# Moving a kernel's SBUF tiles to multiples of 256 bytes: padding and pool order in a hybrid encoder layer

## The chip, the cores and the metric

The kernel runs on one core of a Trainium2 chip. The metric is the device time of one execution in microseconds (us). Three runs of the kernel before gave 811.33, 809.4 and 811.11 us, so the median is 811.11 us; a change is called faster or slower where it differs from no change by more than about 0.3 per cent, 2.4 us.

## What is computed

One layer of an encoder for 256 tokens of width 1024, in float32: a half-step SwiGLU network, then a projection that feeds a multi-head latent attention (MLA) and a bidirectional state-space scan (SSD), whose gated results are added back, and a second half-step SwiGLU network.

```python
def reference(x, ...):
    x = x + 0.5 * swiglu(rmsnorm(x, ffn1_norm[l]), ffn1_w_gate[l], ffn1_w_up[l], ffn1_w_down[l])
    h = rmsnorm(x, mix_norm[l])
    u = h @ w_in[l]
    c_q, c_kv, k_pe, z, xbc, dt_f, dt_b, g_a, g_b = jnp.split(u, split_idx, axis=-1)
    a = mla(c_q, c_kv, k_pe, ...)
    m = bi_mamba2(xbc, z, dt_f, dt_b, ...)
    merged = jax.nn.sigmoid(g_a) * (a @ w_attn_branch[l]) + jax.nn.sigmoid(g_b) * (m @ w_ssm_branch[l])
    x = x + merged @ w_out[l]
    x = x + 0.5 * swiglu(rmsnorm(x, ffn2_norm[l]), ffn2_w_gate[l], ffn2_w_up[l], ffn2_w_down[l])
    return x
```

swiglu(h) is (silu(h @ w_gate) * (h @ w_up)) @ w_down, with 2816 hidden columns.

## The kernel before

**Layout.** Activations lie transposed: a tile has 128 partitions (features) and 256 tokens along them. All large products have a weight block of 128 x 128 as the stationary operand, which LDWEIGHTS puts into TensorE, and the activations as the moving operand of a MATMUL.

**Splitting.** TensorE reads float32r here, and to keep float32 accuracy every operand is split in two parts, hi and lo, and a product is the sum of three: hi by hi, hi by lo and lo by hi. An activation's two parts lie side by side, 256 columns of hi and then 256 of lo, in tiles with the axes [P, k, 2, T]: xs (normed input of a stage), hs (hidden activations of a feed-forward network) and ms (output of the state-space scan). Each k takes 2048 bytes of a partition. `wload` (L112 to L125) brings a weight block by DMA into one of four buffers raw, ScalarE copies it into one of four buffers whi (through `copy`, L94) and VectorE puts raw minus whi into one of four buffers wlo (through `tt`, L97). Three pairs of tensors for the first part of the input projection are loaded early into a pool of their own, pre.

**Two matmul loops.** `wstat` (L135 to L143) issues three MATMULs of 256 columns for each weight block: whi by hi (L141), whi by lo (L142), wlo by hi (L143), and each has its own LDWEIGHTS. It makes the input projection (ps_in0 from pre, with the xs of the mixing norm; ps_in1 from whi and wlo), the attention branch (ps_ab), the second half of the scan's branch (ps_sb, which reads ms) and the output projection (ps_o2, which the profile shows as ps_o). `wstat2` (L145 to L156) issues two for each block: wlo by hi, 256 columns (L153, or L156 for the first block of a sum), and whi by hi and lo at once, 512 columns (L154). It makes the two feed-forward networks (ps_gu and ps_d) and the gates and the first half of the scan's branch (ps_half). Here one block's work in `wstat` is called a triple, and in `wstat2` a pair; each covers 768 columns.

**Order of the work.** First network (22 blocks f of ps_gu, then 8 blocks d of ps_d), input projection, then a plan of attention heads, scan pairs and projections that is sorted by hand-set keys, the branches, the output projection, the second network. Each engine works through its own queue in program order; the DMAs of weights are issued by SP.

**Where tiles lie.** Pools take space in a partition from below in the order in which they are opened, and pools with side="right" from above. In the kernel before the pool const is opened first (L81), and raw, w, x, xn and small follow. Later come h and ev (feed-forward networks), or mix and then m0 or attn (mixing part), and from above pre, or ssd in its place. ms and mpb are the last tiles taken from mix (L508 and L509). A tile's buffers are a multiple of 256 bytes apart for raw, whi, wlo, xs, hs and ms (4352, 4352, 4352, 16384, 45056 and 16384 bytes).

Of the kernel before, what the change touches and what calls it, by code (L numbers as in the profile page):

```python
# [8 lines left out]
F32 = mybir.dt.float32  # L9
F32R = mybir.dt.float32r  # L10
# [5 lines left out]
P = 128  # L16
T = 256
# [5 lines left out]


RAWB, WB = 4, 4
NMM, NPL, NG = 3, 2, 3
EB, PRB, QKB = 4, 2, 2

# [44 lines left out]
def build(ctx, tc, A, out, dbg=None):  # L73
# [4 lines left out]
    def pool(name, bufs=1, **kw):  # L78
        return tc.tile_pool(name=name, bufs=bufs, **kw)

    cp = ctx.enter_context(pool("const"))  # L81
    rawp = ctx.enter_context(pool("raw", RAWB))
    wp = ctx.enter_context(pool("w", WB))
    xp = ctx.enter_context(pool("x"))
    xnp = ctx.enter_context(pool("xn", 2))
    sm = ctx.enter_context(pool("small", 2))

    def dump(name, ap):
        if name in dbg:
            nc.sync.dma_start(dbg[name], ap)  # L90
# [120 lines left out]
    def xn_tiles():  # L211
        return xnp.tile([P, KD, 2, T], F32R, tag="xs", name="xs")
# [164 lines left out]
    with ExitStack() as es:  # L377
        mp = es.enter_context(pool("mix", reuse_waits="tile"))
# [7 lines left out]
            return ps_g.tile([P, 512], F32, tag="g", name=name)  # L386


        cqh = mp.tile([P, 3, T], F32R, name="cqh")
        cql = mp.tile([P, 3, T], F32R, name="cql")  # L390
        ckh = mp.tile([P, 2, T], F32R, name="ckh")
# [113 lines left out]
        dump("acs", acs)  # L505

        as_ = xn_tiles()
        ms = mp.tile([P, 8, 2, T], F32R, name="ms")  # L508
        mpb = mp.tile([P, 8, T], F32, name="mpb")  # L509

        m0_es.close()
        at_es = es.enter_context(ExitStack())
# [392 lines left out]
```

## Time and profile before

| | us |
|---|---|
| median of three runs | 811.11 |
| the profiled execution | 809.85 |
| its span, first to last instruction | 808.1 |
| TensorE matmul (PE) busy | 786.8 |
| VectorE (DVE) busy | 625.0 |
| ScalarE (ACT) busy | 493.6 |

The profiled execution took 1.75 us more than its span and 1.26 us less than the median. PE is TensorE with its MATMULs, PEld its LDWEIGHTS, which overlap them. A MATMUL is shown from its start to a modelled end, and the next begins before that end; so the pace of a stream of MATMULs is read from the distance of their starts, not from the busy time or from the duration of one. Names such as ps_gu<-xs,whi are the tile written, then the tiles read.

### The profile page before, as it was taken

How to read it: one execution, taken by the hardware profiler on the slowest of the kernel's cores; microseconds unless marked ns; L12 is line 12 of the kernel's file. 1: busy time of each engine (PE TensorE's matmuls, PEld its weight loads, DVE VectorE, ACT ScalarE, POOL GpSimd, SP SyncE). 2: the span in 40 equal slices, each digit the busy share in tenths (PEclk: the TensorE clock that was granted, in tenths of full speed). 3: DMA queues.
4: the chain of work that ended last, by engine and by line, in shares of the span. 5: the costliest groups of instructions: out<-in, count | busy, mean ns of one | idle time of the engine just before them, and what ended most of it. 6: DMA issues, size and time to landing. Idle time of an engine off the chain costs nothing.

```text
span 808.1 us, 13739 instructions
## 1 busy us (share of the span) xinstructions
PE 786.8 (97%) x5232; PEld 700.4 (87%) x5232; DVE 625.0 (77%) x1276; ACT 493.6 (61%) x866; POOL 0.2 (0%) x4
## 2 busy tenths in 40 slices
PE   5999999999998999999999999999999999999998
PEld 4888888888998998988988887888998888888887
DVE  5899987667797986897898678767787877777553
ACT  6667665555367659569667675567455655655442
POOL 0000000000000000000000000000000000000000
PEclk9999999999999999999999999999999999999999
DMA  7667774667134443322325514441755465564772
GB/s 262 207 196 241 237 237 145 180 187 233 40 104 162 132 135 103 108 79 89 100 82 159 176 54 146 137 135 56 232 172 191 161 204 181 189 188 138 197 211 75
DMA packets 39090, 126.46 MB, mean 156 GB/s; under 512 B 4464, under 2 KB 5872, under 8 KB 39024
## 3 DMA queue, kind: packets, MB, share of 16 engines
q1 hardware_dynamic: 38592, 124.69, 48.6%
q10 hardware_dynamic: 432, 0.89, 0.3%
q8 instruction: 41, 0.67, 0.3%
q14 instruction: 25, 0.20, 0.1%
HBM read 124.52 MB, written 1.05 MB: 155 GB/s over the span
## 4 chain that ended last, share of the span: by engine, by line
PE 87%; DVE 6%; ACT 5%; issue 1%; DMA 1%; ACTq 0%
PE ps_gu L154 20%; PE ps_d L154 10%; PE ps_gu L153 9%; PE ps_half L154 5%; PE ps_d L153 5%; PE ps_in L142 4%; PE ps_in L143 4%; PE ps_in L141 4%; PE ps_y L700 3%; PE ps_half L153 2%; PE ps_sc L613 2%; PE ps_o L640 1%; PE ps_gu L156 1%; PE ps_pl L682 1%; DVE wlo L97 1%; PE ps_pT L630 1%
## 5 line engine op out<-in xcount | busy, mean ns | idle before, releaser
L97 DVE TENSOR_TENSOR wlo<-raw,whi 128x1024 fp32r<-128x1024 f32 (+4 forms) x256 | 289.1, 1131 | 75.5 <-ACT whi L94 74.6
L94 ACT ACTIVATE whi<-raw 128x1024 fp32r<-128x1024 f32 (+4 forms) x256 | 251.6, 986 | 145.4 <-PE ps_d L154 51.2
L154 PE MATMUL ps_gu<-xs,whi 128*128 128x512 f32 x704 | 243.8, 400 | 7.8 <-DVE xs L100 7.7
L153 PE MATMUL ps_gu<-xs,wlo 128*128 128x256 f32 x616 | 173.3, 281 | 1.8 <-DVE wlo L97 1.8
L154 PEld LDWEIGHTS ps_gu<-xs,whi 128*128 128x128 f32 x704 | 127.2, 190 | 32.2 <-ACT whi L94 7.2
L153 PEld LDWEIGHTS ps_gu<-xs,wlo 128*128 128x128 f32 x616 | 117.4, 191 | 6.4 <-DVE wlo L97 2.3
L154 PE MATMUL ps_d<-hs,whi 128*128 128x512 f32 x352 | 122.5, 393 | 0.0
L142 PE MATMUL ps_in<-xs,whi 128*128 128x256 f32 x368 | 105.3, 286 | 0.6 <-DVE xs L100 0.6
L143 PE MATMUL ps_in<-xs,wlo 128*128 128x256 f32 x368 | 105.0, 285 | 0.0
L141 PE MATMUL ps_in<-xs,whi 128*128 128x256 f32 x368 | 104.3, 283 | 0.0
L153 PE MATMUL ps_d<-hs,wlo 128*128 128x256 f32 x336 | 94.7, 282 | 0.0
L154 PEld LDWEIGHTS ps_d<-hs,whi 128*128 128x128 f32 x352 | 65.2, 188 | 13.8
L142 PEld LDWEIGHTS ps_in<-xs,whi 128*128 128x128 f32 x368 | 70.1, 190 | 1.2 <-DVE xs L100 0.8
L143 PEld LDWEIGHTS ps_in<-xs,wlo 128*128 128x128 f32 x368 | 70.1, 191 | 0.5 <-issue 0.3
L141 PEld LDWEIGHTS ps_in<-xs,whi 128*128 128x128 f32 x368 | 70.1, 190 | 0.1
L153 PEld LDWEIGHTS ps_d<-hs,wlo 128*128 128x128 f32 x336 | 63.1, 188 | 0.7
L94 ACT ACTIVATE gu<-ps_gu 128x512 f32<-128x512 f32 x44 | 26.1, 592 | 35.0 <-PE ps_gu L154 35.0
L100 DVE SCALAR_TENSOR_TENSOR xz<-ps_in,vec,xz 128x254 f32<-128x254 f32 (+1 forms) x96 | 44.7, 475 | 1.6 <-ACT xz L530 0.9
L154 PE MATMUL ps_half<-xs,whi 128*128 128x512 f32 x128 | 44.9, 399 | 0.0
L97 DVE TENSOR_TENSOR gu<-ps_gu,gu 128x512 f32<-128x512 f32 x44 | 30.3, 688 | 16.5 <-ACT gu L94 15.9
L97 DVE TENSOR_TENSOR E<-E,cb 128x512 f32<-128x512 f32 x48 | 32.0, 685 | 2.4 <-ACT E L691 1.5
L276 ACT ACTIVATE sg<-gu 128x256 f32<-128x256 f32 x44 | 18.1, 416 | 24.4 <-DVE gu L97 24.3
(232 smaller groups left out, 1375.5 us busy)
## 6 DMA issues: line engine op xcount, KB each, us to landing
raw<-in_w_gu SPq DMA_DIRECT2D x86, 512.0 KB, 3.9
raw<-in_w_in SPq DMA_DIRECT2D x62, 512.0 KB, 4.1
raw<-in_w_d SPq DMA_DIRECT2D x32, 384.0 KB, 3.2
raw<-in_w_d SPq DMA_DIRECT2D x32, 320.0 KB, 3.4
raw<-in_w_sb SPq DMA_DIRECT2D x16, 512.0 KB, 4.2
raw<-in_w_qkv SPq DMA_DIRECT2D x8, 544.0 KB, 3.8
raw<-in_w_ab SPq DMA_DIRECT2D x8, 512.0 KB, 3.8
raw<-in_w_o SPq DMA_DIRECT2D x8, 512.0 KB, 3.8
```

The costliest lines, as they stand in the source:

```text
L94: S.activation(dst, src, AF.Copy, scale=scale)
L97: V.tensor_tensor(out=dst, in0=a, in1=b, op=op)
L100: V.scalar_tensor_tensor(out=dst, in0=a, scalar=s, in1=b, op0=op0, op1=op1)
L141: TE.matmul(ps, pc.hi[:, w], xh, start=first and i == 0, stop=False)
L142: TE.matmul(ps, pc.hi[:, w], xl, start=False, stop=False)
L143: TE.matmul(ps, pc.lo[:, w], xh, start=False, stop=last and i == len(ks) - 1)
L153: TE.matmul(ps[:, 0], pc.lo[:, w], xs[:, k0 + i, 0], start=False, stop=False)
L154: TE.matmul(ps, pc.hi[:, w], xs[:, k0 + i], start=a, stop=b)
L156: TE.matmul(ps[:, 0], pc.lo[:, w], xs[:, k0 + i, 0], start=False, stop=False)
L276: S.activation(sg, gu[:, 0], AF.Silu)
L613: TE.matmul(sc[:, t * T:(t + 1) * T], qk[:HD, t * P:(t + 1) * P], qk[:HD, T:2 * T], start=True, stop=True)
L700: TE.matmul(py[64 * j:64 * j + 64, a:b], st[c, d][:, hh_], M[i][:, j, a:b], start=n == 0, stop=n == 3)
```

## The change

Two pools of padding are opened, below raw (96 floats, 384 bytes of each partition) and behind small (120 floats), and one at the right side (8 floats, 32 bytes). The pool const moves behind the pool xn. In the pool mix, ms and mpb become the first tiles. Nothing else is changed: every engine has the same instructions in the same order with the same waits, and only their addresses differ.

```diff
+PAD0, PAD1, PAD2 = 96, 120, 8
...
-    cp = ctx.enter_context(pool("const"))
+
+    ctx.enter_context(pool("pad0")).tile([P, PAD0], F32, name="pad0")
     rawp = ctx.enter_context(pool("raw", RAWB))
     wp = ctx.enter_context(pool("w", WB))
     xp = ctx.enter_context(pool("x"))
     xnp = ctx.enter_context(pool("xn", 2))
+    cp = ctx.enter_context(pool("const"))
     sm = ctx.enter_context(pool("small", 2))
+    ctx.enter_context(pool("pad1")).tile([P, PAD1], F32, name="pad1")
+    ctx.enter_context(pool("pad2", side="right")).tile([P, PAD2], F32, name="pad2")
...
+        ms = mp.tile([P, 8, 2, T], F32R, name="ms")
+        mpb = mp.tile([P, 8, T], F32, name="mpb")
         cqh = mp.tile([P, 3, T], F32R, name="cqh")
...
         as_ = xn_tiles()
-        ms = mp.tile([P, 8, 2, T], F32R, name="ms")
-        mpb = mp.tile([P, 8, T], F32, name="mpb")
```

The first buffer of each tile, in bytes from the start of a partition, and the remainder after division by 256:

| tile | before | remainder | after | remainder |
|---|---|---|---|---|
| raw | 25632 | 32 | 16896 | 0 |
| whi | 43040 | 32 | 34304 | 0 |
| wlo | 60448 | 32 | 51712 | 0 |
| x | 77856 | 32 | 69120 | 0 |
| xs | 86048 | 32 | 77312 | 0 |
| hs | 124064 | 160 | 124928 | 0 |
| ms | 138304 | 64 | 124928 | 0 |
| mpb | 154688 | 64 | 141312 | 0 |
| cqh, cql, ckh, ckl | 124064 and up | 160 | 149504 and up | 0 |
| whi, wlo of pre | 180192, 204768 | 224 | 180160, 204736 | 192 |
| xz, xd, E of the scan | 186336 and up | 224 | 186304 and up | 192 |
| eye, msk4 | 22816, 23328 | 32 | 116384, 116896 | 160 |
| st1, st2 | 136256, 137280 | 64 | 161696, 162720 | 160 |
| nacc, nsq | 118816, 119840 | 32 | 119200, 120224 | 160 |
| gu of the networks | 169120 | 160 | 169984 | 0 |

## The prediction

> **What bounds the kernel now.** I read the page first: its busy times and the chain that ended last.
>
> ```profile
> PE 786.8 (97%) x5232; PEld 700.4 (87%) x5232; DVE 625.0 (77%) x1276; ACT 493.6 (61%) x866; POOL 0.2 (0%) x4
> ...
> PEclk9999999999999999999999999999999999999999
> ...
> PE 87%; DVE 6%; ACT 5%; issue 1%; DMA 1%; ACTq 0%
> ```
>
> TensorE works in 97% of the span, makes up 87% of the chain, and its clock is granted in full in every slice. So what the change is worth hangs on the pace at which matmuls follow each other; transfers, ScalarE and VectorE lie beside them. The view of the groups gives the counts of the streams that the change touches.
>
> ```profile
> L154 PE MATMUL ps_gu<-xs,whi 128*128 128x512 f32 x704 | 243.8, 400 | 7.8 <-DVE xs L100 7.7
> L154 PE MATMUL ps_d<-hs,whi 128*128 128x512 f32 x352 | 122.5, 393 | 0.0
> L142 PE MATMUL ps_in<-xs,whi 128*128 128x256 f32 x368 | 105.3, 286 | 0.6 <-DVE xs L100 0.6
> L154 PE MATMUL ps_half<-xs,whi 128*128 128x512 f32 x128 | 44.9, 399 | 0.0
> L154 PE MATMUL ps_half<-ms,whi 128*128 128x512 f32 x64 | 21.9, 393 | 0.0
> L142 PE MATMUL ps_ab<-xs,whi 128*128 128x256 f32 x64 | 18.2, 286 | 0.0
> L142 PE MATMUL ps_o<-xs,whi 128*128 128x256 f32 x64 | 18.1, 283 | 0.0
> L142 PE MATMUL ps_sb<-ms,whi 128*128 128x256 f32 x64 | 17.8, 278 | 0.0
> ```
>
> L154 is issued once in a pair: 704 + 352 + 128 + 64 = 1248 pairs. L142 is issued once in a triple: 368 + 64 + 64 + 64 = 560 triples. The idle time before them is next to nothing, but the durations are modelled and overlap, so they don't give a pace. The pace comes from the timeline, from starts one whole tile apart. First `wstat`, with 24 matmuls from one row to the next: ps_o, whose moving operand xs starts 32 bytes behind a multiple of 256; then ps_sb, with the same code and the same buffers whi and wlo, whose moving operand ms starts 64 bytes behind one; then ps_in0, with xs at 32 but weights from pre, at 224.
>
> ```profile
> 604.98 0.28 PE L141 MATMUL ps_o<-xs,whi 128*128 128x256 f32 x1
> ...
> 610.74 0.28 PE L141 MATMUL ps_o<-xs,whi 128*128 128x256 f32 x1
> ```
>
> ```profile
> 572.76 0.28 PE L141 MATMUL ps_sb<-ms,whi 128*128 128x256 f32 x1
> ...
> 578.41 0.28 PE L141 MATMUL ps_sb<-ms,whi 128*128 128x256 f32 x1
> ```
>
> ```profile
> 209.49 0.28 PE L141 MATMUL ps_in<-xs,whi 128*128 128x256 f32 x1
> ...
> 212.32 0.28 PE L141 MATMUL ps_in<-xs,whi 128*128 128x256 f32 x1
> ```
>
> ps_o: 5.76 us over 48 matmuls, 120.0 ns each, 360 ns a triple. ps_sb: 5.65 us over 48, 117.7 ns, 353 a triple. ps_in0: 2.83 us over 24, 117.9 ns, 354 a triple. The work is the same and the addresses differ; the pace differs by 2%. That is the one thing in this trace that says an address matters at all.
>
> Now `wstat2`. L156 comes once for each sum, so its starts are 8 pairs apart in ps_gu and ps_half, and 22 in ps_d.
>
> ```profile
> 120.59 0.28 PE L156 MATMUL ps_gu<-xs,wlo 128*128 128x256 f32 x1
> 123.36 0.28 PE L156 MATMUL ps_gu<-xs,wlo 128*128 128x256 f32 x1
> 126.19 0.28 PE L156 MATMUL ps_gu<-xs,wlo 128*128 128x256 f32 x1
> ```
>
> ```profile
> 152.78 0.28 PE L156 MATMUL ps_d<-hs,wlo 128*128 128x256 f32 x1
> 160.49 0.28 PE L156 MATMUL ps_d<-hs,wlo 128*128 128x256 f32 x1
> ```
>
> ```profile
> 435.29 0.28 PE L156 MATMUL ps_half<-ms,wlo 128*128 128x256 f32 x1
> ...
> 452.05 0.28 PE L156 MATMUL ps_half<-ms,wlo 128*128 128x256 f32 x1
> ```
>
> ps_gu takes turns: 2.77 us for one sum, 2.83 us for the next, so 346.3 and 353.8 ns a pair, 350.0 in the mean, at addresses that are equal modulo 256 throughout. ps_d: 7.71 / 22 = 350.5. ps_half with ms: 16.76 us over 48 pairs, 349.2. So here the start of the moving operand (32, 160, 64) hardly shows, while the same stream has two paces of its own.
>
> **The change, part by part.** *Instructions.* Nothing is added, removed or moved, and no wait changes; all that can change is how fast an instruction runs at its new address.
>
> *The triples.* ms, at 64, is the only moving operand of a split product that starts at a multiple of 64 bytes before. After the change xs, hs and ms all do. I take the pace of the nearest row, ps_sb's 117.7, for all triples that now go at 120.0: the 560, less 64 of ps_sb, less 48 of ps_in0 (6 tiles of 8 blocks), which have the lower pace already. That is 448 x 3 = 1344 matmuls x 2.3 ns = 3.1 us, all on the path, since TensorE doesn't wait in these stretches. The bounds: no gain, if the pace follows something else; and below nothing, if the 192 matmuls of ps_sb lose their lead, + 192 x 2.3 = 0.4 us.
>
> *The pairs.* By the same rule they take the pace of ps_half with ms, 349.2. (704 + 128) x 0.8 + 352 x 1.3 = 0.7 + 0.5 = 1.1 us. The 128 pairs of ps_half with xs are counted like ps_gu, whose operand they share. The bounds are ps_gu's own two paces. If all go at 346.3: 832 x 3.7 + 352 x 4.2 + 64 x 2.9 = 3.1 + 1.5 + 0.2 = 4.7 us less. If all go at 353.8: 832 x 3.8 + 352 x 3.3 + 64 x 4.6 = 3.2 + 1.2 + 0.3 = 4.6 us more. I take the value of ms, since it is the only row with an operand of the new kind.
>
> *The weights.* whi and wlo start at 32 modulo 64 everywhere in this trace (pre at 224 too), so no row shows a load of a block that starts at a multiple of 64. I take nothing for it; as a bound towards faster I take as much again as for the moving operand, and as a bound towards slower the pace 353.8 above.
>
> *The tiles the change doesn't reach.* pre and the scan's tiles go from 224 to 192, eye, msk4, st1 and st2 end at 160, and the attention's small tiles stay off 256. ps_in0, the one split product among the readers of pre, runs at the lower pace already. I take nothing for them.
>
> *VectorE and ScalarE.* Do their instructions depend on the start? Operations of one size:
>
> ```profile
> L97 DVE TENSOR_TENSOR sg<-sg,gu 128x256 f32<-128x256 f32 x44 | 18.3, 419 | 3.8 <-ACT sg L276 3.8
> L97 DVE TENSOR_TENSOR nacc<-nacc,nsq 128x256 f32<-128x256 f32 x21 | 8.8, 418 | 0.5 <-ACT nsq L236 0.4
> L97 DVE TENSOR_TENSOR mpb<-mpb,gt 128x256 f32<-128x256 f32 x16 | 5.7, 420 | 0.1
> ```
>
> sg starts at 160, nacc at 32, mpb at 64, and they take 419, 418 and 420 ns: no. For ScalarE I assume the same. And can they keep up with a faster TensorE? The tightest long stretch, from the windows:
>
> ```profile
> 40.00:136.00 96.00, 96.00 (x551) 83.66 (x550) 85.12 (x123) 63.99 (x99) 0.00 (x0) 1.00 0.67 214
> ```
>
> VectorE (the figure ahead of x123) is busy 85.12 of 96 us, ScalarE (ahead of x99) 63.99. A stretch that is 1% shorter leaves VectorE nearly 10 us to spare, so it does not become the bound.
>
> *Transfers.* The raw buffers and x, too, start elsewhere. Weight blocks arrive ahead of need. Only x is waited for:
>
> ```profile
> 1.65 7.54 DMA x<-in_xt
> ```
>
> No row shows the same transfer at two starts, so I take nothing; one hundredth of this piece, either way, would be 0.08 us.
>
> *The sum.* 3.1 + 1.1 = 4.2 us less. The profiled execution of 809.85 us (a span of 808.1 and 1.75 around it) would become 805.6; the median of 811.11 us lies 1.26 above that execution and would become 806.9, 0.5% less.
>
> **The rivals.** *It is the relative start, not the multiple (no difference).* ps_o's triples, at 120.0, have a moving operand at 32 and weights at 32, so both start at the same place modulo 256. ps_sb has 64 and 32, ps_in0 32 and 224: both differ, and they run at 117.7 and 117.9. After the change xs, whi and wlo stand at 0, again the same place, so ps_in1, ps_ab, ps_o and ps_gu keep their pace, and ms joins them at 0: + 192 x 2.3 ns = 0.4 us, plus 64 pairs x 0.8 = 0.05. That gives 811.6 us. For it speaks ps_in0, which is fast though both its operands start at 32 modulo 64; this is the strongest row against my forecast. Against it speaks ps_d, at 160 with weights at 32, which is no faster than ps_gu's mean. [...]
>
> *The slow beat everywhere (slower).* ps_gu shows that one stream at fixed addresses has two paces, and that it goes over from the one to the other at each new sum. Which of them a stream falls into may follow from how the reads of the weights and of the moving operand meet. With all three operands at the same place modulo 256 all pairs may settle at 353.8 and all triples at 120.0: 4.6 + 0.4 = 5.0 us more, 816.1 us. It decides from the point where more than half of the pairs that now go faster stay at 353.8, since then 2.4 us are lost. For it speaks that ps_o, with the same place for both, is locked at 120.0; against it, that ps_gu has both operands at 32 as well and is locked only half of the time.
>
> *The fast beat everywhere.* The far end of my own case: pairs at 346.3 and triples at 117.7, 4.7 + 3.1 = 7.8 us less, 803.3 us. It needs ps_gu to lose its slow turn altogether.
>
> **How the numbers follow.** The forecast with its far end has a chance of 0.45: 806.9 us, and by itself 803 to 809. No difference has 0.36, slower 0.19. The measurement tells 0.3%, 2.4 us, from no change; the forecast's 4.2 lies outside of that, the relative start inside, the slow beat outside. The range: at the low end twice the forecast's gain, for weight loads that gain as much as the moving operand, 2 x 4.2 = 8.4 us, 802.7, rounded down to 802; at the high end the slow beat, cut short a little at 815. About one in ten is left out on each side.
>
> **What would show it right or wrong.** In the profile after: starts of ps_o's L141 24 matmuls apart by 2.82 to 2.83 us instead of 2.88 is the forecast's first term; by 2.88 still, with ps_sb up from 2.82 to 2.88, is the relative start. In ps_gu, L156 every 2.79 us in the mean is the second term; 2.77 each time is the fast beat, 2.83 each time the slow one. ps_in0 should stay at 2.83. VectorE's 418 to 420 ns and the transfer of x should stay. The prediction is wrong if the pace of the streams stays and the time moves, for then something else depends on the address; or if weight loads at 0 give a pace outside of 346 to 354 a pair, which no row of before shows.

## The result and the profile after

| | before | after |
|---|---|---|
| median of 20 runs, us | 809.73 | 810.61 |
| lowest and highest | 808.43, 811.35 | 809.59, 812.46 |
| span of the profiled execution | 808.1 | 808.6 |

The ratio is 1.0013 with a 95% interval of 1.0007 to 1.0019: 0.9 us more, which lies within the 0.3 per cent that count as no difference. Forecast were 4.2 us less. (The median of three runs that the forecast started from, 811.11, lies 1.4 us above that of twenty; this moves the forecast time, not the difference.)

The page of the kernel after has TensorE in the same place: busy in 97% of the span, its clock granted in full (0.999 in the mean).

```profile
span 808.6 us, 13739 instructions
...
PE 787.4 (97%) x5232; PEld 699.9 (87%) x5232; DVE 625.3 (77%) x1276; ACT 493.9 (61%) x866; POOL 0.2 (0%) x4
...
PEclk9999999999999999999999999999999999999999
```

So the pace of the streams decides here too. The timeline of the kernel after, first for triples (L147 is their first MATMUL; 24 matmuls are 8 triples): ps_in0, ps_sb, ps_o.

```profile
209.35 0.28 PE L147 MATMUL ps_in<-xs,whi 128*128 128x256 f32 x1
...
212.07 0.28 PE L147 MATMUL ps_in<-xs,whi 128*128 128x256 f32 x1
...
572.08 0.28 PE L147 MATMUL ps_sb<-ms,whi 128*128 128x256 f32 x1
...
577.84 0.28 PE L147 MATMUL ps_sb<-ms,whi 128*128 128x256 f32 x1
...
604.70 0.28 PE L147 MATMUL ps_o<-xs,whi 128*128 128x256 f32 x1
...
610.46 0.28 PE L147 MATMUL ps_o<-xs,whi 128*128 128x256 f32 x1
```

ps_o: 5.76 us over 48 matmuls, 120.0 ns each, as before. ps_sb: 5.76 over 48, 120.0, up from 117.7. ps_in0: 2.72 over 24, 113.3, down from 117.9; nothing before the change went as fast. Now the pairs (L162, once in each sum): ps_gu 8 pairs apart, ps_d 22, ps_half with ms 48 from the first row to the last.

```profile
119.79 0.28 PE L162 MATMUL ps_gu<-xs,wlo 128*128 128x256 f32 x1
122.56 0.28 PE L162 MATMUL ps_gu<-xs,wlo 128*128 128x256 f32 x1
125.38 0.28 PE L162 MATMUL ps_gu<-xs,wlo 128*128 128x256 f32 x1
...
151.96 0.28 PE L162 MATMUL ps_d<-hs,wlo 128*128 128x256 f32 x1
159.72 0.28 PE L162 MATMUL ps_d<-hs,wlo 128*128 128x256 f32 x1
...
434.96 0.28 PE L162 MATMUL ps_half<-ms,wlo 128*128 128x256 f32 x1
...
451.74 0.28 PE L162 MATMUL ps_half<-ms,wlo 128*128 128x256 f32 x1
```

ps_gu still takes turns at 2.77 and 2.82. ps_d has 7.76 / 22 = 352.7 ns a pair in place of 350.5, ps_half 16.78 / 48 = 349.6 in place of 349.2.

To see whether this makes up the time, I take for each stream the mean distance from each start to the next (distances over 300 ns, which are waits, left out), times three for a triple and summed over both matmuls for a pair. Where a number below is called a mean, it is this one; it holds the short pauses between sums too.

| stream | count | before, ns | after, ns | difference, us |
|---|---|---|---|---|
| ps_d, first and second network | 176, 176 pairs | 350.3, 350.3 | 352.2, 353.1 | +0.3, +0.5 |
| ps_sb | 64 triples | 353.4 | 360.0 | +0.4 |
| ps_in0 | 48 triples | 357.4 | 348.5 | -0.4 |
| ps_half with ms | 64 pairs | 349.1 | 349.8 | 0.0 |
| ps_gu, first and second network | 352, 352 pairs | 352.0, 349.6 | 351.8, 349.5 | -0.1, 0.0 |
| ps_in1 | 320 triples | 367.5 | 367.1 | -0.1 |
| ps_ab | 64 triples | 365.6 | 365.7 | 0.0 |
| ps_o | 64 triples | 363.4 | 363.4 | 0.0 |

The sum is 0.6 us more, beside the 0.9 of the medians and the 0.5 between the two profiled spans. Four streams changed their pace. In three of them (ps_d, ps_sb, ps_half with ms) the operand moved relative to its weights; ps_in0 kept its distance and fell into another rhythm. The streams whose operand and weights moved together (xs with whi and wlo) kept it.

### The profile page after: what moved, and what is told of

Its sections match the earlier page's. It is cut to its first block, busy times and chain, and to the rows that moved or that the text cites. A ratio compares the mean times of both kernels' runs of the same rounds, so it can differ in the third digit from the quotient of the medians.

```text
span 808.6 us, 13739 instructions
## 1 busy us (share of the span) xinstructions
PE 787.4 (97%) x5232; PEld 699.9 (87%) x5232; DVE 625.3 (77%) x1276; ACT 493.9 (61%) x866; POOL 0.2 (0%) x4
## 4 chain that ended last, share of the span: by engine, by line
PE 85%; DVE 7%; ACT 6%; issue 1%; DMA 1%; ACTq 0%
PE ps_gu L160 20%; PE ps_d L160 10%; PE ps_gu L159 9%; PE ps_half L160 5%; PE ps_d L159 5%; PE ps_in L148 4%; PE ps_in L149 4%; PE ps_in L147 3%; PE ps_y L706 3%; PE ps_half L159 2%; PE ps_sc L619 2%; DVE wlo L103 1%; PE ps_o L646 1%; PE ps_gu L162 1%; PE ps_pT L636 1%
## 5 line engine op out<-in xcount | busy, mean ns | idle before, releaser
L160 PE MATMUL ps_d<-hs,whi 128*128 128x512 f32 x352 | 123.3, 398 | 0.0
L147 PE MATMUL ps_in<-xs,whi 128*128 128x256 f32 x368 | 104.2, 283 | 0.0
L147 PEld LDWEIGHTS ps_in<-xs,whi 128*128 128x128 f32 x368 | 70.0, 190 | 0.1
```

The costliest lines, as they stand in the source:

```text
L147: TE.matmul(ps, pc.hi[:, w], xh, start=first and i == 0, stop=False)
L160: TE.matmul(ps, pc.hi[:, w], xs[:, k0 + i], start=a, stop=b)
```

## The experiments

Three theories stood at the start. *Relative start*: what counts is the distance, modulo 256 bytes, from the start of the weights to the start of the moving operand, and a distance of 0 is a slow case. *Multiple*: the forecast's reason, a start at a multiple of 64 or 256 is faster by itself. *Chance*: a stream falls into one of its rhythms whatever its starts.

**Starts alone.** A kernel of only triples and pairs, in sections that take any start (in bytes modulo 256: moving operand, whi, wlo). The layer is left out. This kernel and the three others of sections ran once each.

```python
SECS = [('t', 0, 0, 0), ('p', 0, 0, 0), ('t', 4, 0, 0), ..., ('t', 32, 32, 32), ('p', 32, 32, 32), ...]
```

> The kernel leaves out the layer: it loads x, two tiles of weights and one of moving data, runs sections of split matmuls in the loops' own forms (triples of three 256-column matmuls, pairs of 256 and 512) at chosen starts, and writes x out. Theory R (relative start: the pace follows the distance, modulo 256 bytes, between the start of the moving operand and that of the weights): triples at distance 0 go at 120.0 ns a matmul, with both operands at 0 and with both at 32 alike; distances 32 and 64 give 118 or less, with weights at 0 and at 32 alike. Theory M (multiple: a start at a multiple of 64 is faster by itself, the forecast): both at 0 is faster than both at 32, by about 2 ns a matmul, and starts of 4, 8, 16 and 32 are slower than 0. Theory N (starts don't matter, the paces are a state that a stream falls into): all sections agree within 0.5 ns or differ without order, and the repeated sections at 0 and 128 don't repeat. Pairs: R expects 350 at distance 0, and leaves open whether another distance gives less than 346; with a transfer running beside them, R expects the same paces.

The timeline of this kernel: the first MATMUL of a triple (L121), 21 matmuls apart in each couple of rows. In this order: all at 0; all at 32; moving operand at 64 with weights at 32; moving operand at 64, whi at 0, wlo at 128. Last, a section of 48 matmuls, each of whose weight loads reads one column over and over; the column lies 4 bytes further on in each of the 8 blocks, so it starts at 0 to 28.

```profile
156.15 0.28 PE L121 MATMUL ps_t<-mv,whi 128*128 128x256 f32 x1
158.67 0.28 PE L121 MATMUL ps_t<-mv,whi 128*128 128x256 f32 x1
...
167.49 0.28 PE L121 MATMUL ps_t<-mv,whi 128*128 128x256 f32 x1
170.01 0.28 PE L121 MATMUL ps_t<-mv,whi 128*128 128x256 f32 x1
...
178.77 0.28 PE L121 MATMUL ps_t<-mv,whi 128*128 128x256 f32 x1
181.21 0.28 PE L121 MATMUL ps_t<-mv,whi 128*128 128x256 f32 x1
...
195.28 0.28 PE L121 MATMUL ps_t<-mv,whi 128*128 128x256 f32 x1
197.65 0.28 PE L121 MATMUL ps_t<-mv,whi 128*128 128x256 f32 x1
...
209.56 5.66 PE L132 MATMUL ps_b<-mv,whi 128*128 128x256 f32 x48
```

2.52 / 21 = 120.0 ns with all three at 0, and the same with all three at 32: the multiple doesn't count. 2.44 / 21 = 116.2 at a distance of 32 with the operand at a multiple of 64; with the operand at 32 and the weights at 0 the same distance gives nearly the same (table), so the operand needs no multiple of 64. 112.9 in the fourth section; (5.66 - 0.28) / 47 = 114.5 with the single column, where the moving operand and its start are those of the 120.0. The paces by distance, both weights at 0, in the first place of each (for 0, whose first place is the first section of the kernel, in the second). For triples it is the pace over 21 matmuls in the second half of the section, for pairs the mean over the section.

| distance, bytes | 0 | 4 | 8 | 16 | 32 | 64 | 96 | 128 | 160 | 192 | 224 |
|---|---|---|---|---|---|---|---|---|---|---|---|
| triples, ns a matmul | 120.0 | 123.4 | 120.0 | 118.6 | 116.9 | 117.8 | 119.9 | 118.8 | 117.4 | 117.8 | 118.4 |
| pairs, ns a pair | 349.5 | 359.7 | 351.6 | 346.9 | 349.1 | 349.6 | 350.3 | 349.9 | 348.2 | 351.9 | 351.5 |

The multiple falls. For triples a distance of 0 is slow, but not alone in that: 4 is slower, 8 and 96 are as slow. Not every distance repeats: 128 came again at 120.0 and then 118.7, and 32 at 117.8, so the strict form of the relative start was in doubt from here on. For pairs 0 is not slow in the mean. In all three later sections at 0 or at 32 throughout they have two paces, 352 in the first half and 347 in the second, much like ps_gu's two turns.

The sections at the end that were meant to have transfers beside them had none. The page shows the share of the DMA engines in 40 slices of 6.3 us:

```profile
DMA  7999989778600000000000000000000000000000
```

From some 70 us on (11 slices) the share is under a tenth, and these sections lie behind 221 us. What the kernel shows instead is that the first places of 4 to 32 ran beside transfers (123.4 at 4, 116.9 at 32), and that in the repeats below, without any, 4 and 32 have 123.2 to 123.4 and 116.6 to 116.9: transfers left these paces as they are.

**The kernel after with a distance of 64.** One pad moves xs, hs and ms to 64, and pre to 0, so that its distance stays 64.

```diff
-PAD0, PAD1, PAD2 = 96, 120, 8
+PAD0, PAD1, PAD2, PADX = 96, 120, 56, 16
+    ctx.enter_context(pool("padx")).tile([P, PADX], F32, name="padx")
     xnp = ctx.enter_context(pool("xn", 2))
```

> The kernel after, with xs, hs, ms and the tiles behind them 64 bytes further on, so that every split product has its moving operand 64 bytes behind its weights modulo 256 (weights at 0, pre at 0 too). R: the triples of ps_in1, ps_ab, ps_sb and ps_o go from 120.0 to 118 ns a matmul or to the 113.3 that ps_in0 has at this distance in the kernel after: 512 triples x 3 x 2.2 to 6.7 ns, so 3.4 to 10.3 us less than after, and pairs change by an unknown amount between +4.6 and -4.7 us; in all 0.990 to 0.998 of before. M: starts are multiples of 64 in both kernels, so the time is that of after, ratio 1.001. N: within 0.998 to 1.002 without a pattern in the streams.

807.84 us, ratio to the kernel before 0.9978 [0.9968, 0.9987]. ps_sb has its 353.3 again, ps_in1 came from 367.1 to 361.5, ps_ab to 360.2, ps_o to 345.8 in the mean. The gain lies at the low end of what was expected. The timeline shows ps_o in the rhythm of 113.3: 2.72 us over 24 matmuls.

```profile
602.77 0.28 PE L148 MATMUL ps_o<-xs,whi 128*128 128x256 f32 x1
...
605.49 0.28 PE L148 MATMUL ps_o<-xs,whi 128*128 128x256 f32 x1
```

**A distance of 128.** The same edit with PADX = 32.

> As rel64, with a distance of 128 bytes modulo 256. R: ps_d and all pairs take the 350.5 ns that ps_d has at this distance in the kernel before; for triples no row shows this distance, anything between 113 and 120 ns a matmul; in all 0.988 to 1.001 of before. M: 1.001 as after. N: within 0.998 to 1.002.

809.8 us, ratio 1.0 [0.9992, 1.0009]. ps_sb 355.9, ps_o 360.0, ps_ab 362.4, ps_d 350.3 and 351.1. These triples lie between those at 0 and at 64, so the distance is more than a matter of zero or not.

**Undoing one part.** The kernel after, with hs back at a distance of 128 and ms at 32, as before the change; xs and the weights stay at 0.

```diff
+            es.enter_context(pool("padh")).tile([P, 32], F32, name="padh")
             hp = es.enter_context(pool("h", reuse_waits="tile"))
...
+        es.enter_context(pool("padm")).tile([P, 8], F32, name="padm")
```

> The kernel after with hs 128 and ms 32 bytes further on, so that these two have the distance to the weights that they have in the kernel before, while every absolute start differs. R: ps_sb goes back from 120.0 to 117.7 ns a matmul (0.4 us), ps_d back from its two paces to 350.5 a pair, ps_half with ms to 349.2; the time is that of before, ratio 0.9995 to 1.0005. M: hs and ms lose what the multiple gives them or nothing; ms at 32 is off a multiple of 64, so ps_sb stays at 120.0 and the ratio at 1.001. N: 1.000 to 1.002.

809.39 us, ratio 1.0005 [0.9996, 1.0014]. The interval alone can't tell 1.0 from the 1.0013 of the change; the streams can. ps_sb in the timeline:

```profile
572.38 0.28 PE L147 MATMUL ps_sb<-ms,whi 128*128 128x256 f32 x1
...
578.04 0.28 PE L147 MATMUL ps_sb<-ms,whi 128*128 128x256 f32 x1
```

5.66 / 48 = 117.9 again, and the means of ps_d (350.3, 350.3), ps_half with ms (349.1) and ps_sb (353.4) are those of before to the tenth of a nanosecond, though hs and ms lie at other addresses, one of them (hs, at 128) at a multiple of 128. So the losses of ps_d and ps_sb came from their starts relative to the weights.

**All triples.** Sections as in the first kernel, for a grid of starts of the moving operand and of wlo; the layer is left out.

> The kernel leaves out the layer and runs sections of triples: whi at 0, wlo at 0, 32, ... 224 and the moving operand at 0, 16, 32, ... 224 modulo 256, 72 sections. Theory R: each section keeps one pace and the sections with the same three starts as in m1_starts repeat it (0/0/0 at 120.0 ns a matmul; moving 64 and wlo 0 at 117.8; moving 64 and wlo 128 at 113.3; moving 128 and wlo 64 at 116.5 to 118); a stream whose three starts lie well apart goes at about 113. Theory N (the 113.3 of one section was a state that it fell into by chance): the 113.3 doesn't repeat, or turns up without regard to the starts.

All at 0 gave 120.0 once more. But 64/0/0 (moving operand, whi, wlo) went at 113.3 where the first kernel had 117.8, and 64/0/128 at 118.7 where that had 113.3; 128/0/64, expected at 116.5 to 118, went at 120.0. At a distance other than 0 the starts alone don't fix the rhythm: the strict form of the relative start falls. The 113.3 also came at 16/0/128 and 192/0/128. That starts well apart go at some 113 was expected and failed: 57 of the 72 sections lie at 117.6 to 119.1, and of the ten at 119.9 or more only one has all its starts at one place.

**All pairs.** The same for pairs.

> The same grid with sections of pairs. R: sections repeat m1_starts (0/0/0 at 352, moving 16 and wlo 0 at 346.9, moving 64 and wlo 128 at 352), and the whole grid lies between 344 and 356 ns a pair, since only one weight load falls into the long matmul. N: a spread of 8 ns or more between repeats of one combination.

It couldn't compare starts at the usual pace. All of its 1434 us went by at under a third of it: a MATMUL of 256 columns took 0.42 us of the timeline and one of 512 took 0.84.

```profile
700.29 0.73 PE L126 MATMUL ps_p<-mv,wlo 128*128 128x256 f32 x1
700.71 1.15 PE L127 MATMUL ps_p<-mv,whi 128*128 128x512 f32 x1
701.55 0.73 PE L126 MATMUL ps_p<-mv,wlo 128*128 128x256 f32 x1
```

```profile
core 0: 1434.4 us, clock 1.000
```

This 1.000 is no reading. The page of this run has no PEclk row, since its trace holds no record of the clock, and the same 1.000 is given for the kernel of repeats below, which has no record either and ran at the usual pace. In the first kernel, where the granted clock was 0.55 from 218 to 225 us (0.987 in the mean of the run), MATMULs of 256 columns came 0.213 us apart. 0.42 is twice that, so an estimate from these two numbers is a clock at a quarter; no record shows it. In nearly all sections a pair took 1234 ns, whatever the starts: at this pace they made no visible difference.

**wlo 128 bytes away from whi.** The kernel with a distance of 64, and the buffers of wlo in a pool of their own, at 128 modulo 256.

```diff
+    ctx.enter_context(pool("padl")).tile([P, 32], F32, name="padl")
+    wl = ctx.enter_context(pool("wl", WB))
+    ctx.enter_context(pool("padm")).tile([P, 32], F32, name="padm")
...
-            lo = (pl or wp).tile([P, 1024 if pl else 1088], F32R, tag="wlo", name="wlo")
+            lo = (pl or wl).tile([P, 1024 if pl else 1088], F32R, tag="wlo", name="wlo")
```

> The kernel rel64 with the four buffers wlo 128 bytes further on than whi modulo 256, as in the section of m1_starts that went at 113.3 ns. R: ps_in1, ps_ab, ps_sb and ps_o go at 113.3 ns a matmul, 340 a triple, instead of 118 to 120: 448 x 20 + 64 x 13 ns = 9.8 us less than before; the pairs, at 350 to 352, cost 0 to 2.6 us: 0.988 to 0.992 of before. N: 0.996 to 1.000, as rel64 or before.

803.62 us, ratio 0.9912 [0.9895, 0.9928]: faster than both kernels. But not by the steps expected. Against the kernel with a distance of 64 (means), ps_gu came from 352.7 and 350.2 to 349.2 and 346.7, ps_d from 351.0 and 351.1 to 346.7 and 346.6, ps_half with ms from 350.4 to 346.7: 704 x 3.5 + 352 x 4.4 + 64 x 3.7 = 2.5 + 1.5 + 0.2 = 4.2 us from pairs. The triples, for which it was made, gave some 0.4 us together: ps_in1 came from 361.5 to 357.6 (1.2 us), ps_o stayed near 346 (346.3), ps_sb and ps_ab were slower by 3.3 and 2.3 ns, and ps_in0, whose starts had not changed, went from 348.3 to 357.6 and took back 0.4 us. The timeline of ps_d:

```profile
143.92 0.28 PE L166 MATMUL ps_d<-hs,wlo 128*128 128x256 f32 x1
...
151.54 0.28 PE L166 MATMUL ps_d<-hs,wlo 128*128 128x256 f32 x1
```

7.62 / 22 = 346.4, the pace of ps_gu's fast turn, now in every sum of ps_d.

**Repeats.** Twenty kinds of sections, four times each in a mixed order, to see what is fixed; the layer is left out.

> The kernel leaves out the layer and runs ten combinations of starts as triples and as pairs, each four times in mixed order. R in its strict form (the three starts modulo 256 set the pace): each combination repeats within 0.5 ns a matmul. R in a looser form (the distance sets which rhythms are open to a stream, and what ran before picks one): moving, whi and wlo at one start always 120.0; a distance of 4 bytes always slowest, about 123.4 and 359 a pair; the others between 112 and 120, and the distance of 64, which went at 117.8 in m1_starts and at 113.3 in m2_triples, shows both. N: 120.0 turns up at other distances as often as at 0, or 0 leaves it. For pairs, which m3_pairs could not tell since TensorE ran at under a third of its pace throughout: 352 at 0, 347 at 16, 359 at 4, if the order doesn't matter.

The timeline: triples at a distance of 0, 4 and, for 192/0/128, the first of its four places; 21 matmuls each.

```profile
109.82 0.28 PE L121 MATMUL ps_t<-mv,whi 128*128 128x256 f32 x1
112.34 0.28 PE L121 MATMUL ps_t<-mv,whi 128*128 128x256 f32 x1
...
70.08 0.29 PE L121 MATMUL ps_t<-mv,whi 128*128 128x256 f32 x1
72.67 0.29 PE L121 MATMUL ps_t<-mv,whi 128*128 128x256 f32 x1
...
58.77 0.28 PE L121 MATMUL ps_t<-mv,whi 128*128 128x256 f32 x1
61.15 0.28 PE L121 MATMUL ps_t<-mv,whi 128*128 128x256 f32 x1
```

2.52 / 21 = 120.0, 2.59 / 21 = 123.3, 2.38 / 21 = 113.3. In the second half of the section, where a pace has settled, every triple section at 0 was at 120.0, every one at 4 between 123.2 and 123.4, every one at 32 between 116.6 and 116.9, and 192/0/128 at 113.3 all four times. Others changed between places: 64/0/0 had 117.8 three times and 113.4 once, 64/0/128 118.8 to 119.1 three times and 113.3 once, 16/0/128 113.3 three times and 117.8 once, 16/0/0 118.6 twice and 116.8 twice. Of pairs, a distance of 4 gave 358.4 to 359.8, of 16 346.8 to 347.4. At 0 the fast half was now the first, in three of the four sections, and one had the slow pace in both, 352.2 in its mean: which turn is the slow one isn't fixed by the starts either. So a looser form stands: the starts set which rhythms are open (for triples one at 0 and at 192/0/128, two at 64/0/0). That what ran before picks one of several is a guess, which no run shows.

**Distances of 4 and 16 in the whole kernel.** The kernel after with every xs, hs and ms one float, or four floats, behind its multiple of 256.

```diff
+OFF = 1
+    def at_off(pl, k, **kw):
+        t = pl.tile([P, k * 2 * T + 64], F32R, **kw)
+        return t[:, OFF:OFF + k * 2 * T].rearrange("p (k c t) -> p k c t", k=k, c=2)
...
-        return xnp.tile([P, KD, 2, T], F32R, tag="xs", name="xs")
+        return at_off(xnp, KD, tag="xs", name="xs")
```

> The kernel after with xs, hs and ms 4 bytes further on inside longer tiles, weights as they are. R, with the paces of m1_starts at a distance of 4 (123.4 ns a matmul, 359.3 a pair): 1248 pairs x 8 to 9 ns and 512 triples x 10 ns, so 15 to 17 us more than after: 1.019 to 1.023 of before. M: a start off a multiple of 64 costs at most what before and after differ by, 1.00 to 1.01. N: 1.00 to 1.002.

> As off4, with 16 bytes. R, with the paces of m1_starts at a distance of 16 (118.6 ns a matmul, 346.9 a pair): 1248 pairs x 3 to 5 ns and 512 triples x 4 ns less than after, 6 to 8 us: 0.991 to 0.994 of before. M: not faster than after, 1.001 or more. N: 0.998 to 1.002.

A distance of 4: 824.62 us, ratio 1.0185 [1.0169, 1.0201]. A distance of 16: 804.71 us, ratio 0.9943 [0.993, 0.9956]. Both medians lie just short of the effect expected, and both intervals reach into the expected ranges. Twelve bytes are worth 20 us. The timelines of ps_d, first at 4, then at 16:

```profile
141.34 0.28 PE L163 MATMUL ps_d<-hs,wlo 128*128 128x256 f32 x1
149.24 0.29 PE L163 MATMUL ps_d<-hs,wlo 128*128 128x256 f32 x1
```

```profile
144.32 0.28 PE L163 MATMUL ps_d<-hs,wlo 128*128 128x256 f32 x1
151.95 0.28 PE L163 MATMUL ps_d<-hs,wlo 128*128 128x256 f32 x1
```

7.90 / 22 = 359.1 and 7.63 / 22 = 346.8; the sections alone had 359.7 and 346.9. For pairs at these two distances the small kernel foretells the large one.

**The starts that the repeats point to.** The kernel with wlo apart, and xs at 192 in the mixing part alone (the edit shown), or in every part with ms at 192 too; hs at 64 in both.

```diff
-    def xn_tiles():
-        return xnp.tile([P, KD, 2, T], F32R, tag="xs", name="xs")
+    def xn_tiles(off=32):
+        t = xnp.tile([P, KD * 2 * T + 64], F32R, tag="xs", name="xs")
+        return t[:, off:off + KD * 2 * T].rearrange("p (k c t) -> p k c t", k=KD, c=2)
...
-            self.xs = xn_tiles()
+            self.xs = xn_tiles(32 if vcol == V_MIX else 0)
```

> This is the kernel hilo128 with one more edit: in the mixing part xs starts at 192 modulo 256 (weights hi at 0, lo at 128 as in hilo128), and in the two networks it stays at 64; hs and ms stay at 64. In the repeats, triples at 192/0/128 went at 113.3 ns in four of four places. Relative start (looser form: the distance opens rhythms): ps_ab, ps_in1 and ps_o go to about 340 a triple, from 362.5, 357.5 and 346.3 in hilo128: 64 x 22.5 + 320 x 17.5 + 64 x 6.3 = 1.4 + 5.6 + 0.4 = 7.4 us less than hilo128, less some 0.5 for the 128 pairs of ps_half with xs at 192, so about 797 us, a ratio to the kernel before of about 0.983; ps_gu, ps_d, ps_sb and ps_half with ms, whose starts don't change, stay at 346 to 349 a pair and 357 a triple. If the rhythm is a matter of what ran before and not of the starts: ps_in1, ps_ab and ps_o stay between 346 and 362, and the ratio stays at 0.991.

> This is the kernel hilo128 with xs at 192 in every part, ms at 192 and hs kept at 64. Relative start, looser form: triples as in mix192, and ps_sb too at about 340 (64 x 17 = 1.1 us less than hilo128); but ps_gu, whose xs is now at 192, goes at the 350 to 353 a pair that the repeats gave for 192/0/128, in place of 349.2 and 346.7: 704 x about 3.5 = 2.5 us more. Sum about 798.5 us, ratio 0.985, and slower than mix192 by about 1.5 us. If the starts don't set the pace, both kernels are alike at 0.991.

The mixing part alone: 801.73 us, ratio 0.9902 [0.9889, 0.9915], the fastest kernel of the study by its median, though its interval overlaps that of wlo apart (0.9895 to 0.9928). Everything but hs at 192: 804.25 us, 0.9928 [0.9915, 0.9941]. Timelines, first of the one with xs at 64 in the networks (ps_gu, 8 pairs, then ps_sb, 24 matmuls), then of the one with 192 everywhere but in hs (ps_gu, then ps_sb, 48 matmuls):

```profile
119.05 0.28 PE L166 MATMUL ps_gu<-xs,wlo 128*128 128x256 f32 x1
121.83 0.28 PE L166 MATMUL ps_gu<-xs,wlo 128*128 128x256 f32 x1
...
568.28 0.28 PE L151 MATMUL ps_sb<-ms,whi 128*128 128x256 f32 x1
...
571.13 0.28 PE L151 MATMUL ps_sb<-ms,whi 128*128 128x256 f32 x1
```

```profile
121.20 0.28 PE L166 MATMUL ps_gu<-xs,wlo 128*128 128x256 f32 x1
124.01 0.28 PE L166 MATMUL ps_gu<-xs,wlo 128*128 128x256 f32 x1
...
568.47 0.28 PE L151 MATMUL ps_sb<-ms,whi 128*128 128x256 f32 x1
...
573.91 0.28 PE L151 MATMUL ps_sb<-ms,whi 128*128 128x256 f32 x1
```

At 192 ps_gu has 2.81 us a sum in place of 2.78, and ps_sb 5.44 / 48 = 113.3 in place of 2.85 / 24 = 118.8: the same start is right for triples and wrong for pairs, as the repeats had it. The streams whose starts are those of the kernel with wlo apart kept their means within 0.2 ns (ps_d 346.7 and 346.6, ps_gu 349.1 and 346.7, ps_sb 356.6 against 356.7). In runs of eight triples without a pause ps_in1 and ps_ab went at 340 to 350 in both kernels, against 358 to 360 in the kernel after; ps_ab had 357 with wlo apart. The expected 797 was missed by 4.7. In the means ps_ab, ps_in1 and ps_o came to 350.2, 352.6 and 342.6, which is 2.6 us in place of the 7.4: the expectation set the 340 against means of the kernel with wlo apart that hold the pauses between sums, and part of that kernel's ps_in1 was at 340 to 342 already. The ratio, 0.990, lies where it was put for a rhythm that doesn't follow the starts; it is the unbroken runs that speak for the starts. The second kernel missed its 798.5 as well, by 5.8 us, and was slower than the first by 2.5 us where 1.5 were expected.

## Why the prediction was wrong

The measured 810.61 lies inside the range of 802 to 815, but that range was wide enough to hold no change as well; the way of the change and its reason were missed.

*What bounds the kernel* was right: TensorE is busy in 97% before and after, and the means of its streams add up to 0.6 of the 0.9 us.

*The triples*: this step failed, 3.1 of the 4.2 us. It put ps_sb's 117.7 down to its own start at a multiple of 64. Shown in its place: all three at 0 and all three at 32 go alike, at 120.0, and it is the distance to the weights that set ps_sb apart. ps_o, ps_ab and ps_in1 had a distance of 0 before (32 and 32) and have one after (0 and 0), and nothing came of the move; ps_sb lost its distance of 32 and 0.4 us with it. Both are what the rival *It is the relative start, not the multiple* gave, in place, sign and size. The row that the text itself called the strongest against the forecast, ps_in0, fast at 32 with weights at 224, should have had the higher chance.

*The pairs*: failed by the same reason, with the sign too. Instead of 1.1 us less they cost 0.8 more: hs went from a distance of 128 to 0, and ps_d went from 350.3 in both networks to 352.2 and 353.1. The rival missed this as well, since it priced only ms. What it held against itself, that ps_d was no faster than ps_gu's mean, compared two streams that differ in more than the distance: at the same distance of 0, after, ps_d goes at 352.7 and ps_gu at 5.59 / 16 = 349.4. Compared with itself, ps_d gains 2.0 and 2.8 ns a pair by its distance of 128, as the undone part shows.

*The weights*, taken at nothing for a start at a multiple of 64, were right in that no such start matters by itself (120.0 with all three at 0 and with all three at 32). But their starts count for as much as those of the moving operand: from all three at 32, the weights moved to 0 gave 116.9 in place of 120.0, and the moving operand moved to 64 gave 116.2.

*The tiles the change doesn't reach*: ps_in0 was to stay at 2.83 and went to 2.72, with its distance unchanged (32 to 224 before, 0 to 192 after, both 64). The repeats show two rhythms for that distance, 117.8 and 113.4, so a change of rhythm without one of distance is what the runs allow; why it came there is open.

*VectorE and ScalarE*: right for VectorE. The groups of the kernel after, whose starts are now 160 for nacc (32 before) and 0 for mpb (64 before):

```profile
L103 DVE TENSOR_TENSOR sg<-sg,gu 128x256 f32<-128x256 f32 x44 | 18.3, 419 | 3.7 <-ACT sg L282 3.7
L103 DVE TENSOR_TENSOR nacc<-nacc,nsq 128x256 f32<-128x256 f32 x21 | 8.8, 420 | 0.4 <-ACT nsq L242 0.3
L103 DVE TENSOR_TENSOR mpb<-mpb,gt 128x256 f32<-128x256 f32 x16 | 5.7, 420 | 0.1
```

419, 420 and 420 ns beside 419, 418 and 420. ScalarE, for which the same was assumed, is busy for 493.9 us in all, 493.6 before. *Transfers*: the chain of the kernel after names another piece of x.

```profile
0.73 4.30 DMA x<-in_xt
```

That is no matter of the address: in the kernel with a distance of 16, where x starts at the same place as after, the chain has 1.64 and 7.62 us, as before the change.

*The slow beat everywhere* did not come: ps_gu kept its turns. The forecast was 4.2 us less than the median before, and the rival of the relative start 0.5 more; measured were 0.9 more.

What is shown is that the distance between the starts of moving operand and weights, modulo 256, changes the pace of TensorE with nothing else changed. How it does so is not. That reads of the weights and of the moving operand meet is a guess, which no run shows directly. For it speaks the section with one column of weights: the block whose column starts at 0, as the moving operand does, goes at 113 to 114 in the second half (three matmuls) in place of 120.0. The 114.5 of the whole section alone would prove less, since the column starts at 4 to 28 in the other blocks. For it speaks too that the starts made no visible difference where TensorE ran at under a third of its pace (1234 ns a pair in nearly all sections). What picks a rhythm where several are open was not found either.

## What to carry to other kernels

Where TensorE issues one weight load for each MATMUL and is never idle, measure its pace from starts one sum apart, compare streams of one shape, and look at the starts of moving and stationary operand relative to each other before rounding any of them. Putting both at one alignment makes the distance 0, which cost 120.0 ns a matmul here where most others gave 113 to 119; padding costs no instruction (13739 instructions before and after), and the best of these kernels gained 1.0% [0.8, 1.1] by it. Repeat a section in another order before trusting its pace: 64/0/0 had both 117.8 and 113.4. A row that two theories explain differently, such as ps_in0, deserves the weight of the forecast, for a kernel of single sections settles it in one run.

## What the runs showed of the hardware

- A distance of 4 bytes costs triples 2.8% over one of 0 (123.4 against 120.0 a matmul) and pairs as much (359.7 against 349.5), and the whole kernel was 1.9% slower than the kernel before (1.0185). 8 bytes cost triples nothing over 0 (120.0), and 16 bytes gain (118.6, and 346.9 a pair).
- The only starts that always gave triples 113.3 (192/0/128) are not the best of pairs (349.9 to 351.6 there, 346.8 to 347.4 at 16/0/0).
- TensorE ran through a whole kernel of 2304 matmuls at under a third of its pace (0.42 and 0.84 us where other kernels have some 0.12 and 0.23). The clock given for it, 1.000, stands there for want of any record, so a run's page has to be looked through for its PEclk row before that number is believed. The cause is open.
